# Attention of an encoder layer: from a planner's order to one order written by hand

## The chip, the cores and the metric

The kernel runs on one core of a Trainium2 chip. The metric is device time in microseconds of one launch. All matrix products of the attention are fp32r; large values are split into a high part (rounded to fp32r) and a low part (the rest), and three products of parts stand for one exact product.

## The reference

One layer for two groups: a prompt of 2048 frames and a sample of 8 streams with 16 new frames and 1024 cached frames each. Cut to what matters here:

```python
h = rmsnorm(x, norm1_g) * (1 + scale) + shift
z = h @ w_in                                  # conv columns u_a, u_g; q, k, v; forget gate f
u = u_a * sigmoid(u_g)
q, k = rmsnorm(q, q_norm_g), rmsnorm(k, k_norm_g)     # per head: 8 heads of 64
logf = log_sigmoid(f + b_f)
# attention, causal, for the prompt and (with the cache) for the sample
s = q @ k.T * 64 ** -0.5 + (cum_q[:, None] - cum_k[None, :])     # cum = cumsum(logf)
attn = softmax(where(k_pos <= q_pos, s, -1e30)) @ v
# convolution branch: causal depthwise conv, width 31, then LayerNorm over channels and swish
conv_out = silu((y - mean(y)) * rsqrt(var(y) + eps) * ln_g + ln_b)
x = x + g1 * (concat([conv_out, attn]) @ w_out)
x = x + g2 * ((silu(h2 @ w_gate) * (h2 @ w_up)) @ w_down)        # h2: a second modulated rmsnorm of x
```

## The kernel before

The program goes through `project_u_v` (to about 400 us), `project_q_k` (to about 600), `attention` (608 to 1215), `project_out`, and the feed-forward part (from about 1250). A planner orders each engine's instructions: it lists those that can run, by priority (the order in which the program states them, moved by `later`), on a timeline of its own. SyncE (SP) issues most transfers; POOL issued those of keys and queries for the attention.

The attention has 4 head pairs `p` and 4 query blocks `qb` of 512 frames: 16 steps. A step has 4 (qb + 1) key tiles of 128 frames, two heads each; one key tile for one head is a unit, 320 units in all (24 in the first two steps). A unit: two score matmuls into a bank `s` (three banks, tag `u`; lines 948 and 949), a mask matmul on the diagonal (951), an exp on ScalarE (953) into `ef`, the high part `e` on ScalarE (1131, called from `parts_of`), the low part on VectorE or, every third, on POOL (1132), and later three value matmuls into `pv` (939). A column of the value tile that holds ones gives the softmax's sum in the same bank.

The softmax needs each query's maximum before the exp. `score_maxima` computes it ahead: one matmul into a bank `mx` (two banks, tag `cv`; 909, mask 911) and one reduction on VectorE (912) for each query tile and key block, 320 in all. `spread_maxima` transposes a step's maxima (923) and writes them as extra rows of the query operand `Q2` (925), so that the score matmul subtracts them. 32 maxima are computed during `project_q_k`, and later ones up to 48 units ahead.

At a step's end ScalarE copies value and sum out of the banks (970, 971), Ln and Exp give a reciprocal (973, 974), three operations of VectorE refine it and scale the value (975 to 977), and SP writes it to `cat_d` (978). `load` brings the next step's queries and values; a value load `vraw` (883) takes a slot of the ring `ef`.

Beside that runs `background`: the convolution's norm over 5 chunks of frames (`conv_norm`; VectorE's lines 727, 742 and the Newton steps 93 to 95, transfers 708 and 744) and the sample group's attention over 8 streams (`sample_setup` with a bias write of all streams, 1022; `sample_batch`). It uses one PSUM bank, `lane`, and starts after two steps. `weave` deals out these generators in proportion to given counts; a part that `take` runs with a positive `by` has a later priority. `last_parts` finishes the last block of queries and keys (`finish`; the transfers `q_d<-qp` and `k_d<-qp`).

Of the kernel before, what the change touches and what calls it, by code (L numbers as in the profile page):

```python
# [6 lines left out]
F32 = mybir.dt.float32  # L7
# [40 lines left out]
LEAD = 48  # L48
FIRST = 2
BACK = 0.85  # L50
MAXIMA_BY, BACK_BY = -300, 1000
# [66 lines left out]
class Layer:  # L118
# [583 lines left out]
    def conv_norm(self, ch, sp, bank):  # L702
# [7 lines left out]
        def channel_mean(src):  # L710
            pm = bank
            for j in range(4):
                nc.tensor.matmul(pm[32 * j:32 * j + 32, :n], self.ones[:, 0:32], src[j], start=True, stop=True,
                                 tile_position=(0, 32 * j))
            m = sp.tile([P, 512], F32, tag="cm", name="cm")
            nc.scalar.copy(m[:, :n], pm[:, :n])
            po = bank
            nc.tensor.matmul(po[:, :n], self.mean, m[:, :n], start=True, stop=True)
            return po

        mu = channel_mean([y[:, j, :n] for j in range(4)])
        ms = sp.tile([P, 512], F32, tag="cw", name="cmu")
        nc.scalar.copy(ms[:, :n], mu[:, :n])
        yield
        sqs = []
        for j in range(4):
            nc.vector.tensor_tensor(y[:, j, :n], y[:, j, :n], ms[:, :n], ALU.subtract)
            sq = sp.tile([P, 512], F32, tag="cq", name="cq", bufs=4)
            nc.scalar.activation(sq[:, :n], y[:, j, :n], AF.Square)
            sqs.append(sq[:, :n])  # L730
        yield
        var = channel_mean(sqs)
        v = sp.tile([P, 512], F32, tag="cv", name="cvar")[:, :n]
        nc.vector.tensor_scalar(v, var[:, :n], EPS, None, ALU.add)
# [3 lines left out]
        newton_rsqrt(nc, r, sp.tile([P, 512], F32, tag="cm", name="ct")[:, :n], v, 2)  # L738
        yield
        for j in range(4):  # L740
            z = y[:, j, :n]
            nc.vector.tensor_tensor(z, z, r, ALU.mult)
        yield
# [3 lines left out]
    def operands(self):  # L747

        nc, a = self.nc, self.a
        self.bm = self.cst.tile([P, 2, 4], F32, name="bm")  # L750
        nc.sync.dma_start(self.bm, a["bm"])
# [4 lines left out]
        for k, r, v in (("v", slice(AUX, AUX + 8), -1.0), ("t", slice(HD, HD + 2), 1.0)):  # L756
# [16 lines left out]
        yield from self.take(self.maxima_of_all, AHEAD)  # L773

    def attention(self, ctx):
# [4 lines left out]
        self.split3 = 0  # L780
# [5 lines left out]
        for t in self.Vt:  # L786
            for i in range(2):
                nc.scalar.activation(t[:, i, :, 1, :], self.ones[:, 0:HD].unsqueeze(1).broadcast_to([P, 4, HD]), AF.Copy, scale=1.0 - i)
        self.lf_bank = "cv"
        self.after_attention = ctx  # L790
        self.eslots, self.ecount = [(self.awk, f"e{i}") for i in range(5)], 0
        back = self.background()
        nback, done, units, scored = 15 + 5 * 7 + 1 + 8 * 11, 0, 0, AHEAD
        total = sum(8 * (qb + 1) for _, qb in STEPS)
        self.V = {}
        drain(self.load(0))

        for n, (p, qb) in enumerate(STEPS):
            parts = [(self.attend(p, qb, n), 8 * (qb + 1))]
            if n + 1 < len(STEPS):  # L800
                parts.append((self.load(n + 1), 4))
            if n == 0:
                parts.append((self.last_parts(), 12))
            units += 8 * (qb + 1)
            k = units + LEAD - scored
            parts.append((self.take(self.maxima_of_all, k, MAXIMA_BY), k))
            scored += k
            if n >= FIRST:
                k = int(nback * (units - quiet) / (total - quiet) / BACK) + 1 - done
                parts.append((self.take(back, k, BACK_BY), k))  # L810
                done += k
            else:
                quiet = units
            weave(*parts)
        drain(back)

    def take(self, gen, k, by=0):

# [808 lines left out]
```

## Time and profile before

| | |
|---|---|
| runs | 2849.34 us median of 3 (2840.97 to 2852.43) |
| profiled execution | 2841.08 us, span 2839.3, mean granted TensorE clock 0.977 |
| busy in the span | TensorE 96%, VectorE 76%, ScalarE 51%, POOL 18% |
| attention, 608 to 1215 us | TensorE 560.5 of 607 us, VectorE 467.4, ScalarE 427.2, POOL 177.5; clock 0.94 |

In the profile PE is TensorE's matmul, PEld its weight load, DVE VectorE, ACT ScalarE, SP SyncE; a q behind the name is the engine's queue. A row by stretch gives from:to, its length, busy us of each engine with its instruction count, the clock, the share of the DMA engines' time, and GB/s. A row by line gives busy us and mean ns of one, then the idle time of its engine just before it and what ended that. A row of waits gives total us, times and the longest.

### The profile page before, as it was taken

What the parts mean: (1) busy time and instruction counts of PE and PEld (TensorE: products, weight loads), DVE (VectorE), ACT (ScalarE), POOL (GpSimd) and SP (SyncE); (2) the same over time, 40 slices, a digit from 0 to 9 for tenths busy, and PEclk for the clock granted to TensorE, in tenths of its full rate; (3) what the DMA queues carried; (4) which work ended last, traced back from release to release, by engine and by line L of the source; (5) the groups of instructions that cost most, each with busy time, mean ns of one, the idle gap of its engine ahead of it and who ended that gap; (6) DMA issues with size and microseconds to landing.
All of it is one profiled execution on the core that took longest, in us unless ns stands there. A gap on an engine that the chain in (4) does not pass through costs nothing.

```text
span 2839.3 us, 48486 instructions
## 1 busy us (share of the span) xinstructions
PE 2731.4 (96%) x16536; PEld 2525.9 (89%) x16536; DVE 2158.0 (76%) x4235; ACT 1436.9 (51%) x2812; POOL 503.2 (18%) x685
## 2 busy tenths in 40 slices
PE   7999999999988999989998999999999999999999
PEld 6899988866666777789998999999999999999999
DVE  3698898988886888644488899777787778676765
ACT  4543323357675777754354445444454446555552
POOL 3454412243222232213212110000000000000000
PEclk9999999989898999999998999999999999999999
DMA  8753567673346656264667678776786669788873
GB/s 306 258 188 110 187 212 265 187 203 114 82 115 178 188 184 192 87 234 143 213 239 257 216 262 291 251 228 206 233 293 212 218 208 309 247 277 258 280 249 117
DMA packets 390024, 603.23 MB, mean 212 GB/s; under 512 B 46240, under 2 KB 249152, under 8 KB 387728
## 3 DMA queue, kind: packets, MB, share of 16 engines
q1 hardware_dynamic: 375312, 574.72, 62.3%
q0 software_dynamic: 14464, 25.42, 3.7%
q8 instruction: 130, 2.13, 0.3%
q14 instruction: 118, 0.97, 0.1%
HBM read 421.97 MB, written 178.07 MB: 211 GB/s over the span
## 4 chain that ended last, share of the span: by engine, by line
PE 78%; DMA 9%; DVE 5%; issue 4%; ACT 2%; POOL 1%; SPq 1%; POOLq 0%; ACTq 0%; DVEq 0%
PE z L1412 44%; PE z L509 7%; PE pv L939 5%; PE acc L1115 4%; PE pa L319 3%; PE pvv L339 3%; PE pg L319 3%; PE s L948 2%; PE s L949 2%; PE mx L909 2%; DMA vraw<-o_v 1%; DVE M L912 1%; DMA k_d<-qp 1%; PE pu L319 1%; DMA wraw<-w_in 1%
## 5 line engine op out<-in xcount | busy, mean ns | idle before, releaser
L1412 PE MATMUL z<-rT,rW 128*128 128x360 f32 (+1 forms) x8316 | 1382.0, 328 | 4.3 <-ACT oR L1214 2.0
L1412 PEld LDWEIGHTS z<-rT,rW 128*128 128x128 f32 x8316 | 1378.9, 188 | 5.9 <-ACT oR L1214 2.4
L1131 ACT ACTIVATE rW<-rR 128x512 fp32r<-128x512 f32 x714 | 436.1, 618 | 386.4 <-PE z L1412 294.9
L1132 DVE TENSOR_TENSOR rW<-rR,rW 128x512 fp32r<-128x512 f32 x714 | 480.7, 678 | 150.5 <-ACT rW L1131 147.3
L697 DVE SCALAR_TENSOR_TENSOR cv<-cu,cpar,cv 128x384 f32<-128x384 f32 x580 | 311.7, 618 | 2.0 <-ACT cv L695 1.6
L939 PE MATMUL pv<-e,V 128*128 128x512 f32 (+3 forms) x960 | 264.3, 381 | 20.5 <-ACT e L1131 11.4
L912 DVE TENSOR_REDUCE M<-mx 128x1 f32<-128x512 f32 (+2 forms) x320 | 190.2, 606 | 50.5 <-PE mx L909 34.2
L939 PEld LDWEIGHTS pv<-e,V 128*128 128x128 f32 x960 | 168.6, 192 | 64.6 <-ACT e L1131 12.3
L953 ACT ACTIVATE ef<-s 128x512 f32<-128x512 f32 (+3 forms) x320 | 166.3, 530 | 107.0 <-PE s L949 49.2
L509 PE MATMUL z<-hqx,wqh 128*128 128x384 f32 (+1 forms) x768 | 196.5, 333 | 0.8 <-DVE logf L346 0.8
L1131 ACT ACTIVATE rT<-traw 128x360 fp32r<-128x360 f32 (+1 forms) x315 | 149.7, 503 | 89.0 <-DMA traw<-gt_d 58.1
L1132 DVE TENSOR_TENSOR rT<-traw,rT 128x360 fp32r<-128x360 f32 (+1 forms) x315 | 158.6, 537 | 44.9 <-ACT rT L1131 44.6
L1132 POOL TENSOR_TENSOR e<-ef,e 128x512 fp32r<-128x512 f32 (+3 forms) x106 | 128.1, 1209 | 361.8 <-ACT e L1131 170.5
L1132 DVE TENSOR_TENSOR e<-ef,e 128x512 fp32r<-128x512 f32 (+3 forms) x214 | 147.9, 701 | 42.9 <-ACT e L1131 41.6
L1131 ACT ACTIVATE e<-ef 128x512 fp32r<-128x512 f32 (+3 forms) x320 | 175.0, 567 | 4.6
L509 PEld LDWEIGHTS z<-hqx,wqh 128*128 128x128 f32 x768 | 135.7, 188 | 18.7 <-issue 15.5
L909 PE MATMUL mx<-K,Q 96*128 96x512 f32 (+2 forms) x320 | 135.1, 431 | 15.2 <-DVE M L912 12.9
L1115 PE MATMUL acc<-ch,woh 128*128 128x360 f32 (+1 forms) x384 | 122.6, 338 | 16.1 <-ACT ch L1131 8.2
L1340 DVE TENSOR_TENSOR rR<-rR 128x512 f32<-128x512 f32 (+1 forms) x136 | 93.1, 705 | 54.9 <-DMA rR<-w_down 50.6
L948 PE MATMUL s<-Q,K 128*128 128x512 f32 (+3 forms) x320 | 127.3, 399 | 1.9 <-ACT ef L953 1.8
L1115 PE MATMUL acc<-ch,wol 128*128 128x360 f32 (+1 forms) x384 | 127.7, 336 | 0.0
L509 PE MATMUL z<-hqx,wql 128*128 128x384 f32 (+1 forms) x384 | 126.4, 329 | 0.0
(306 smaller groups left out, 3958.7 us busy)
## 6 DMA issues: line engine op xcount, KB each, us to landing
rR<-sup_d SPq DMA_DIRECT2D x176, 256.0 KB
rR<-w_gate SPq DMA_DIRECT2D x132, 256.0 KB
traw<-gt_d SPq DMA_DIRECT2D x154, 180.0 KB
rR<-w_down SPq DMA_DIRECT2D x104, 256.0 KB
rR<-sdn_d SPq DMA_DIRECT2D x96, 256.0 KB
rR<-w_up SPq DMA_DIRECT2D x88, 256.0 KB
sup_d<-rR SPq DMA_DIRECT2D x88, 256.0 KB
wa<-w_ada SPq DMA_DIRECT2D x16, 1024.0 KB
```

The source lines that it names most:

```text
L319: nc.tensor.matmul(pz[:, :n], w[:, m], x[:, :n], start=(c == 0 and k == 0), stop=(c == CB - 1 and k == 2))
L509: nc.tensor.matmul(z[:, :n], w[:, m], x[:, :n], start=(c == 0 and k == 0), stop=(c == CB - 1 and k == 2))
L697: self.pin(nc.vector.scalar_tensor_tensor(dst, src, w, acc[i], ALU.mult, ALU.add))
L909: nc.tensor.matmul(mx[:, :w], Q2[0:AUX, h, j * P:(j + 1) * P], K2[kb][0:AUX, h, :w], start=True, stop=not diag)
L912: nc.vector.tensor_reduce(M[:, i, kb:kb + 1], mx[:, :w], AX.X, ALU.max)
L939: nc.tensor.matmul(z[h][:, off:], V[kt // 4][:, v, kt % 4, h:h + 2, :].rearrange("p b c -> p (b c)"), e[:, x, off:], start=(kt == 0 and i ...
L948: nc.tensor.matmul(s[:, off:], K1[kb][:, h, sl], Q1[:, h, off:], start=True, stop=False)
L953: nc.scalar.activation(ef[:, off:], s[:, off:], AF.Exp)
L1115: self.nc.tensor.matmul(z[:, :n], w[:, m], y, start=(first and i == 0 and k == 0), stop=(last and i == len(terms) - 1 and k == 2))
L1131: self.nc.scalar.activation(hi, raw, AF.Copy)
L1132: engine.tensor_tensor(lo, raw, f32(hi), ALU.subtract)
L1412: nc.tensor.matmul(z, W[:, x, m], t[:, y, :w], start=(k == 0 and i == 0), stop=(k == n - 1 and i == 2))
```

## The change

The four compute engines follow the order in which the program states the attention; SP stays with the planner. The loop goes over units: scores and exp of unit u, one maximum (two until 44 are ahead), the low part of unit u - 1, the values of unit u - 5 (u - 2 in the first 25 units), one step of each finishing block, and the side work's due parts. The side work is cut into 266 parts (it has new `yield`s) and starts after 24 units; in these, the last block of `project_q_k` is finished.

A step's end is a generator, `normalize`: ScalarE copies the two banks whole (`zc`), moves the sums to the other half of the partitions by two transfers on its own queue, and three of the remaining multiplies and the write to `cat_d` go to POOL. The maxima reach `Q2` by a copy of 8 rows and 8 transfers of one row instead of two products with `bm`; K then has one row of -1 instead of eight. Keys and queries are loaded on SP. Value loads have a slot of their own (`vr`). There are 4 + 4 slots `e` instead of 5 + 3, and three cache slots `kv` for keys and values of the sample instead of two and two. The convolution's last taps are issued before the stream.

```diff
-LEAD = 48
-FIRST = 2
-BACK = 0.85
-MAXIMA_BY, BACK_BY = -300, 1000
+LEAD = 44
+FIRST = 24
+BACK = 266
+ENGINES = {mybir.EngineType.PE, mybir.EngineType.Activation, mybir.EngineType.DVE, mybir.EngineType.Pool}
...
     def attention(self, ctx):
...
-        back = self.background()
...
-        for n, (p, qb) in enumerate(STEPS):
-            parts = [(self.attend(p, qb, n), 8 * (qb + 1))]
...
-            weave(*parts)
-        drain(back)
+        self.conv_part(999, TT)
+        drain(self.load(0))
+        with self.tc.manual_schedule(engines=ENGINES):
+            self.stream()
+
+    def stream(self):
+        units = [(n, p, qb, kt, h) for n, (p, qb) in enumerate(STEPS) for kt in range(4 * qb + 4) for h in range(2)]
+        back = self.background()
+        scored, done, ended, late = AHEAD, 0, None, None
+        for u, (n, p, qb, kt, h) in enumerate(units):
+            if kt == h == 0:
+                step = (p, qb, self.V[p], [])
+                loads = self.load(n + 1) if n + 1 < len(STEPS) else iter(())
+            ef, off, e = self.scores(n, p, qb, kt, h)
+            for _ in range(2):
+                if scored < u + 1 + LEAD:
+                    next(self.maxima_of_all, 0)
+                    scored += 1
+            if late:
+                self.low_part(*late)
+            late = (e[:, 1, off:], ef[:, off:], f32(e[:, 0, off:]))
+            self.waiting.append((step, kt, h, off, e))
+            while len(self.waiting) > len(self.eslots) // 2 + (u > FIRST):
+                self.value(*self.waiting.pop(0))
+            for g in self.finishing[:]:
+                if next(g, 1):
+                    self.finishing.remove(g)
+            if kt % (2 * qb + 2) == 1 and h == 0:
+                next(loads, 0)
+            if u < FIRST:
+                self.parts(0, TT)
+            else:
+                while not ended and done < BACK * (u - FIRST) / (len(units) - FIRST - 8):
+                    ended = next(back, 1)
+                    done += 1
...
     def keys(self, p):
...
-            nc.gpsimd.dma_start(K2[0:HD + 2], rows[HD:])
+            nc.sync.dma_start(f32(K2[0:HD + 2]), rows[HD:])
...
     def spread_maxima(self, Z, Q2):
...
-        for h in range(2):
-            nc.vector.tensor_tensor(Q2[r, h, :].rearrange("r (j q) -> r j q", j=4),
-                                    pz[r, :].unsqueeze(1).broadcast_to([8, 4, P]),
-                                    self.bm[r, h, :].unsqueeze(2).broadcast_to([8, 4, P]), ALU.mult)
+        yield
+        m = self.lp.tile([P, P], F32R, tag="mrow", name="mrow", bufs=2)
+        nc.vector.tensor_copy(m[r], pz[r])
+        for i in range(8):
+            nc.sync.dma_start(f32(Q2[AUX:AUX + 1, i // 4, i % 4 * P:(i % 4 + 1) * P]), f32(m[AUX + i:AUX + i + 1]))
+        yield
...
+    def normalize(self, p, qb, zc):
+        nc, wk = self.nc, self.awk
+        sm, r = (wk.tile([P, 512], F32, tag=k, name=k, bufs=1) for k in ("sm", "rs"))
         for h in range(2):
             o, x = slice(HD * h, HD * h + HD), slice(HD - HD * h, P - HD * h)
-            nc.scalar.copy(sm[o], z[h][x])
-            nc.scalar.copy(pvs[o], z[h][o])
...
+            nc.scalar.dma_start(sm[o], zc[x, h])
+            yield
+        yield
+        nc.scalar.activation(r, sm, AF.Ln, scale=-1.0)
         self.last_exp = nc.scalar.activation(r, r, AF.Exp, scale=-1.0)
-        nc.vector.tensor_tensor(sm, sm, r, ALU.mult)
-        nc.vector.scalar_tensor_tensor(sm, sm, 2.0, r, ALU.subtract, ALU.mult)
-        nc.vector.scalar_tensor_tensor(pvs, pvs, -1.0, sm, ALU.mult, ALU.mult)
-        nc.sync.dma_start(self.cat_d[:, 4 + p, qb * 512:(qb + 1) * 512], pvs)
+        yield
+        nc.gpsimd.tensor_tensor(sm, sm, r, ALU.mult)
+        yield
+        yield
+        nc.vector.scalar_tensor_tensor(r, sm, 2.0, r, ALU.add, ALU.mult)
+        yield
+        for h in range(2):
+            o = slice(HD * h, HD * h + HD)
+            nc.gpsimd.tensor_tensor(zc[o, h], zc[o, h], r[o], ALU.mult)
+            nc.gpsimd.dma_start(self.cat_d[o, 4 + p, qb * 512:(qb + 1) * 512], zc[o, h])
...
     def sample_batch(self, b, bank):
...
             if c < 2:
-                kt = self.smc.tile([P, NP, 512], F32, tag="kc", name="kc")
+                kt = self.smc.tile([P, 4 * DC], F32, tag="kv", name="kc").rearrange("p (g k) -> p g k", g=NP)
                 nc.sync.dma_start(kt, a["kcT"][b, :, :, c0:c0 + w])
```

More of the change, by code (lines that the diff above doesn't have):

```diff
@@ L737, in conv_norm @@
         nc.scalar.activation(r, r, AF.Exp, scale=-0.5)
[L738 removed]
         yield
+        for _ in range(2):
+            newton_rsqrt(nc, r, sp.tile([P, 512], F32, tag="cm", name="ct")[:, :n], v, 1)
+            yield
         for j in range(4):
@@ L772, in operands @@
         self.maxima_of_all = self.score_maxima()
-        yield from self.take(self.maxima_of_all, AHEAD)
+        for _ in range(AHEAD):
+            next(self.maxima_of_all)
+            yield
     def attention(self, ctx):
@@ L815, in attention @@
-        drain(back)
-    def take(self, gen, k, by=0):
-        for _ in range(k):
-            with later(self.tc, by):
-                end = next(gen, 1)
-            if end:
-                return
-            yield
-    def last_parts(self):
-        while self.todo:
-            self.parts(0, TT)
-            yield
+        self.eslots, self.ecount = [(self.awk, f"e{i}") for i in range(4)], 0
+        self.V, self.finishing = {}, []
+        self.conv_part(999, TT)
+        drain(self.load(0))
@@ new lines, in attention @@
+        with self.tc.manual_schedule(engines=ENGINES):
+            self.stream()
+    def stream(self):
+        units = [(n, p, qb, kt, h) for n, (p, qb) in enumerate(STEPS) for kt in range(4 * qb + 4) for h in range(2)]
+        back = self.background()
+        scored, done, ended, late = AHEAD, 0, None, None
[4 more added lines that the diff above has]
+            ef, off, e = self.scores(n, p, qb, kt, h)
+            for _ in range(2):
+                if scored < u + 1 + LEAD:
[14 more added lines that the diff above has]
+                self.parts(0, TT)
+            else:
+                while not ended and done < BACK * (u - FIRST) / (len(units) - FIRST - 8):
+                    ended = next(back, 1)
+                    done += 1
+        self.low_part(*late)
+        for w in self.waiting:
+            self.value(*w)
+        for g in self.finishing:
+            drain(g)
+        assert ended or next(back, 1), "parts are left"
@@ new lines, in value @@
+    def value(self, step, kt, h, off, e):
+        nc = self.nc
+        p, qb, V, z = step
+        last = kt == 4 * qb + 3
+        if kt == 0:
+            z.append(self.bank("tr", "pv"))
+        for i, (v, x) in enumerate(((0, 0), (0, 1), (1, 0))):
+            nc.tensor.matmul(z[h][:, off:], V[kt // 4][:, v, kt % 4, h:h + 2, :].rearrange("p b c -> p (b c)"), e[:, x, off:],
+                             start=(kt == 0 and i == 0), stop=(last and i == 2))
+        if last:
+            if h == 0:
+                self.zc = self.awk.tile([P, 2, 512], F32, tag="zc", name="zc", bufs=1)
+            nc.scalar.copy(self.zc[:, h], z[h])
+            if h:
+                self.finishing.append(self.normalize(p, qb, self.zc))
```

191 lines of the change are left out of this document (85 added, 106 removed).

## The prediction

> **What bounds the kernel now.** I read the page first: TensorE is busy 96% of the span, so a gain must come from a stage in which this figure hides waiting. The change touches one stage, the attention, from the first score matmul at 608.1 us to the last value matmul at 1212.5. Next I read busy time by stretch of time, for all instructions and for one line that runs once in each unit (a key tile times a query block of one head; 320 in all). The cuts are where the other work changes: before the convolution's norm (24 units done), during it (104 units), from the sample group on (192 units). The changed code cuts nearly there too: its side work starts after unit 24 and 95 of its 266 parts are the norm's.
>
> ```profile
> PE 2731.4 (96%) x16536; PEld 2525.9 (89%) x16536; DVE 2158.0 (76%) x4235; ACT 1436.9 (51%) x2812; POOL 503.2 (18%) x685
> ```
>
> All instructions by stretch, then line 949 (second score matmul), the sample and norm bank `lane`, and line 912 (the maxima's reduction):
>
> ```profile
> core 0: us, PE busy (x) PEld busy (x) DVE busy (x) ACT busy (x) POOL busy (x), PEclk, DMA share, GB/s
> 608.00:662.00 54.00, 48.92 (x192) 34.30 (x192) 44.53 (x75) 33.62 (x75) 28.36 (x32) 0.82 0.71 191
> 662.00:871.00 209.00, 187.91 (x825) 132.76 (x824) 173.65 (x293) 145.03 (x289) 57.51 (x53) 0.93 0.30 86
> 871.00:1215.00 344.00, 323.70 (x2153) 245.18 (x2152) 249.17 (x444) 248.54 (x491) 91.62 (x88) 0.96 0.57 172
> 950.00:1200.00 250.00, 245.29 (x1764) 184.26 (x1764) 194.82 (x339) 192.25 (x385) 67.76 (x64) 1.00 0.52 163
> ...
> 662.00:871.00 209.00, 40.77 (x104) 21.12 (x104) 0.93 0.30 86
> 871.00:1215.00 344.00, 71.48 (x192) 36.67 (x192) 0.96 0.57 172
> 950.00:1200.00 250.00, 53.01 (x145) 27.27 (x146) 1.00 0.52 163
> ...
> 662.00:871.00 209.00, 27.40 (x100) 6.46 (x100) 3.05 (x5) 7.82 (x15) 0.93 0.30 86
> 871.00:1215.00 344.00, 63.04 (x882) 33.74 (x882) 21.05 (x58) 11.34 (x24) 0.96 0.57 172
> ...
> 662.00:871.00 209.00, 67.83 (x113) 0.93 0.30 86
> 871.00:1215.00 344.00, 98.66 (x166) 0.96 0.57 172
> ```
>
> From 950 to 1200 TensorE is busy 98% at clock 1.00 and a unit takes 250/145 = 1.72 us. From 662 to 871 a unit takes 209/104 = 2.01 us, with the clock at 0.93 and no engine over 90%: there the stage waits. For the price of a unit I take a run of three value matmuls, and the score matmul's widths:
>
> ```profile
> 1085.91 0.86 PE L939 MATMUL pv<-e,V 128*128 128x512 f32 x3
> ...
> L939 PE MATMUL pv<-e,V x960: 218/392/792, 621.7 to 1212.5; 128*128 128x512 f32 x137, 128*128 128x256 f32 x20, 128*128 128x384 f32 x19, 128*128 128x128 f32 x16
> L948 PE MATMUL s<-Q,K x320: 220/393/800, 608.1 to 1210.6; 128*128 128x512 f32 x112, 128*128 128x384 f32 x16, 128*128 128x256 f32 x16, 128*128 128x128 f32 x16
> ```
>
> One record lasts 0.39 but the next starts (0.86 - 0.39)/2 = 0.235 us later. Widths of 512 (70%), 384, 256 and 128 (10% each) average 435 columns, so 0.20 us a matmul. A unit has two score and three value matmuls, 1.00, with masks 1.05 (estimate); a maximum costs 0.20, with its mask 0.22. The stage's TensorE work by pitch is then: start 24 x 1.05 + 29 x 0.22 = 32 of 54 us; norm 104 x 1.05 + 113 x 0.22 + 27.4 = 161 of 209; sample 192 x 1.05 + 166 x 0.22 + 63.0 = 301 of 344. So about 22 + 48 + 43 us of 607 are not work; the clock's missing shares (0.18, 0.07, 0.04 of the stretches) are 38 of these. The chain and the waits from 608 to 950 name what ends them:
>
> ```profile
> 621.16 7.09 DMA k_d<-qp
> 789.89 8.46 DMA vraw<-o_v
> 899.18 25.20 DMA vraw<-o_v
> 1218.86 5.85 DMA cat_d<-pvs
> ...
> PEld mx L909 <- DVE M L912: 26.9, 41, 2.8
> ACT V L1131 <- DMA vraw<-o_v: 21.8, 6, 12.6
> PE pv L939 <- ACT e L1131: 11.4, 2, 10.6
> ```
>
> Read: a value load sits in the exp's own ring (tag `ef`, three slots), so a late load holds a slot, ScalarE's split waits up to 12.6 us, and everything behind it in ScalarE's order waits too. The maxima wait for VectorE to empty their two banks.
>
> **The change part by part.** Rows for the prices:
>
> ```profile
> L1132 POOL TENSOR_TENSOR e<-ef,e 128x512 fp32r<-128x512 f32 (+3 forms) x106 | 128.1, 1209 | 361.8 <-ACT e L1131 170.5 <-PE mx L911 55.1 <-PE mx L909 21.3
> L1132 DVE TENSOR_TENSOR e<-ef,e 128x512 fp32r<-128x512 f32 (+3 forms) x214 | 147.9, 701 | 42.9 <-ACT e L1131 41.6
> L925 DVE TENSOR_TENSOR Q<-pz,bm 8x512 fp32r<-8x512 f32 x30 | 19.6, 691 | 2.2 <-PE pz L923 1.9
> L975 DVE TENSOR_TENSOR sm<-sm,rs 128x512 f32<-128x512 f32 x15 | 11.4, 759 | 1.3 <-ACT rs L974 1.1
> L977 DVE SCALAR_TENSOR_TENSOR pvs<-pvs,sm 128x512 f32<-128x512 f32 x15 | 10.2, 683 | 0.0
> L970 ACT COPY sm<-pv 64x512 f32<-64x512 f32 x32 | 18.6, 581 | 10.9 <-PE pv L939 10.3
> L93 DVE SCALAR_TENSOR_TENSOR ct<-cr 128x512 f32<-128x512 f32 (+1 forms) x10 | 7.6, 757 | 0.1
> L1131 ACT ACTIVATE e<-ef 128x512 fp32r<-128x512 f32 (+3 forms) x320 | 175.0, 567 | 4.6
> L953 ACT ACTIVATE ef<-s 128x512 f32<-128x512 f32 (+3 forms) x320 | 166.3, 530 | 107.0 <-PE s L949 49.2 <-PE s L951 24.0 <-DVE e L1132 21.7
> ...
> L1132 DVE TENSOR_TENSOR e<-ef,e x214: 276/681/2440, 611.2 to 1211.8; 128x512 fp32r<-128x512 f32 x75, 128x384 fp32r<-128x384 f32 x12, 128x128 fp32r<-128x128 f32 x10, 128x256 fp32r<-128x256 f32 x10
> L697 DVE SCALAR_TENSOR_TENSOR cu<-uS,cpar,ca x4: 345/348/352, 568.2 to 600.4; 128x128 f32<-128x128 f32 x4
> ...
> Q<-q_d POOLq DMA_DIRECT2D x14, 512.0 KB, 4.7
> K<-k_d POOLq DMA_DIRECT2D x13, 512.0 KB, 6.0
> K<-k_d POOLq DMA_DIRECT2D x11, 264.0 KB, 5.5
> bias_d<-bias SPq DMA_DIRECT2D x1, 4160.0 KB
> ...
> SPq L744 <- DVE cy L742: 88.4, 5, 31.1
> 1096.36 0.34 SPq L978 DMA_DIRECT2D cat_d<-pvs  x1
> ```
>
> *Order.* TensorE, ScalarE, VectorE and POOL follow the written order; SP's queue does not. A unit issues scores, exp, high part, one maximum (two until 44 ahead), the low part of the unit before, the values of five units back, at most one step of a finishing block, 0.92 side parts. Behind each possible wait there is slack: three score banks, two maxima banks, eight `e` slots. ScalarE's and VectorE's latencies for a unit (means of 0.53 and 0.57 for exp and high part, 0.70 or 1.21 for the low part) sum to 2.3 us, against five units of 1.5 us.
>
> *Value load in its own slot.* The 21.8 us of ScalarE's wait goes, provided SP issues the load a step early; late next is VectorE.
>
> *Steps' ends.* Per step VectorE loses two mask products (2 x 0.69), 0.76 and 0.68, and gains one 8-row copy (0.2, estimate): 2.6 us less. ScalarE copies 2 x 0.58 in place of 4 x 0.58 and issues two transfers (0.34 each by SP's row): 0.5 less. POOL takes three multiplies (1.21 each) and two transfer issues; it has 57.5 of 209 us busy, so they hide under its idle time. They may hold VectorE up: its low part takes 0.68 at the median, 2.44 at the longest, and 0.70 in the mean although the mean width asks for 0.68 x 435/512 = 0.58; 214 x 0.12 = 26 us, some 0.2 for each of POOL's 106 low parts. I take 0.2 for each of the 48 new multiplies; bounds 0 and 1.21. Ln now waits for a transfer inside SBUF, two units after its issue.
>
> *Loads of K and Q on SP.* POOL loses 42 issues, SP gains them and 8 one-row transfers a step: 128 x 0.34 = 44 us of queue time, beside work of other engines as long as nothing in front waits. But SP does wait for others (88.4 us on the norm's results), and what stands behind waits too.
>
> *Side work in 266 parts.* Same instructions, but each part ends where another engine must act, so an in-order engine rarely waits for it. VectorE's lumps stay: a Newton part is three operations of 0.76.
>
> *Small things.* The ring of three shared cache slots in place of four, the convolution drained before the stream (its last instruction runs at 600.4 already), one row of -1 in K, signs turned: nothing on the path; if the cache ring is late, a part waits for 1 MB, as in 871 to 950 now.
>
> **The sum.** *Start*: 36 maxima in place of 29, the same chain through `k_d` (7.09): 54 us kept; bounds 45 (VectorE's busy time there now) and 62 (the 7.09 once more). *Norm*: TensorE 104 x 1.05 + 104 x 0.22 + 27.4 = 159. VectorE 173.65, less 9 maxima (0.60 each, 67.83/113) and less 2.6 x 6 to 7 steps: 151. ScalarE 145 less 3. Three engines within 12% of each other in a fixed order leave no room for lumps: six Newton operations and four products behind them, at 0.76 each, put 7.6 us on VectorE in four units, beside 1.06 of its own in each (0.60 and 147.9/320), where TensorE offers 4 x 159/104 = 6.1; of the 5.7 us over, two banks absorb some 2.5; with four large chunks 13 us, and 18 multiplies of POOL at 0.2 make 4: 176, say 177. Bounds: 159 (all hidden) and 209 (as now). *Sample*: 192 x 1.05 + 148 x 0.22 + 63.0 = 297; at the present best rate 192 x 1.72 = 330, less 18 maxima, 326. I take 312, between them: 297, 5 of switching and 10 for one event. The 4160 KB bias write is issued in unit 134; the key block needed by the maximum of unit 140 gets its slot after unit 135 and now queues behind that write (before, on another queue). The value load that stood behind it took 25.20; 5 units are 7.7. So 0 to 18 us late; 10. *Tail*: the step's end is longer by a transfer (4.7 by Q's median) and POOL's products, but only the last two token blocks need it, and SP no longer stands on `cat_d<-pvs` (5.85): 0, bounds -6 and +6.
>
> 54 + 177 + 312 = 543 for 607: 64 us less. The profiled execution took 2841.08 (span 2839.3), 8 below the median 2849.34 and at the lowest run, 2840.97; 2841 - 64 = 2777, and runs of the new kernel should spread likewise: **2780 us**.
>
> Two rules of the Trainium skill bear on the steps' ends. "DMA: Bandwidth & Descriptors", section "Anatomy of one DMA", gives a transfer about 2.0 us of fixed cost plus its bytes at 436 GB/s, so 2.3 us for the 128 KB inside SBUF (an estimate from that page); by that rule Ln, 3.2 us later, never waits, and the slower case below has no price. By the trace's medians of 4.7 to 6.0 Ln waits up to 2.8 us a step, 45 in all, beside three score banks and an idle fifth of ScalarE's time (248.54 of 312); the sum stands by both. "SBUF — State Buffer", section "Who interferes with whom", says that a VectorE instruction with two SBUF inputs contends with a GpSimd instruction that reads SBUF, and that the later one is blocked for the whole of the other; by that rule the upper bound of 1.21 would hold, which is a rival below. The trace's longest of 2.44 agrees, its median of 0.68 does not show it as the rule.
>
> **The rivals.**
> *The floor is reached* (chance 0.20). Start 45, norm 165, sample 300: 510, so 2744. For it: half of the loss is the clock, which returns when gaps are short (1.00 from 950 on). Against: VectorE's lumps.
> *SP's queue takes back half* (0.15). Three late key blocks and three query blocks each have four units of slack, 6 to 7 us, against landings of 5.5 to 6.0 plus what SP waits for in front; 4 us each and 25.2 - 7.7 for the bias write make 42, of which 10 are in the sum: 2812. For it: SP's 88.4. Against: the planner still orders SP's queue by need.
> *POOL shuts VectorE out* (0.08). At 1.21 for each of 18 multiplies VectorE loses 22 us in the norm stretch, not 4: 195 there, and nothing in the sample stretch, where VectorE has 249 of 312: 2780 + 18 = 2798. For it: the 2.44. Against: the mean excess is a tenth of that.
> *It doesn't do what it says* (0.10). The order was never the limit; VectorE stays at 83% in the norm stretch and the sample stretch keeps 1.72 us a unit less its maxima: 54 + 209 + 337 = 600: 2834.
> *Slower* (0.11). Ln waits on ScalarE, in order, for the copy inside SBUF; all exps queue behind it, and three score banks (4.8 us) run dry. Each step then costs landing - 3.2 - 4.8. With 16 steps the gain is gone at a landing of 12 us and the kernel slower by over 0.5% from 13; at 14 it is 2780 + 96 = 2876. For it: 25.20 and 8.46 in the chain. Against: the medians of 4.7 to 6.0, and a queue that nothing else uses.
>
> **How the numbers follow.** The forecast holds 0.36, with a range of its own of 2755 to 2800. A measurement of this kernel tells 0.5% (14 us) from no change. Faster: 0.36 + 0.20 + 0.15 + 0.08 = 0.79; same 0.10; slower 0.11. For 8 in 10 the range is 2735 to 2850: it leaves out the slower case and the lower end of the floor case.
>
> **What would show it.** In the new profile: no wait of ScalarE for `vraw` over 3 us; VectorE's rows for the step's ends gone, POOL's 48 multiplies instead; 104 units from the first `cy` load in some 177 us with VectorE over 85%; granted clock near 1.00 in that stretch; one gap of TensorE of about 10 us near the bias write, ended by K. Wrong if ScalarE's wait for `sm` sums to over 60 us, if TensorE's waits for K or Q sum to over 40, or if the norm stretch keeps over 200 us.

## Result: 4.1% slower

The changed kernel takes 2963.34 us (median of 4, 2959.98 to 2967.66) where the kernel before takes 2846.73 (median of 4): ratio 1.0413, interval 1.0396 to 1.0430. That is 117 us more, where 64 less were forecast. The profiled execution has a span of 2965.9 us.

The profile after. First the page's line of busy time, then the attention by stretch: start, norm, sample, cut at the first load of `cy` and at the end of the last norm chunk. Columns as in the prediction; below them the second score matmul (now line 961) in the same stretches.

```profile
PE 2757.3 (93%) x16536; PEld 2541.1 (86%) x16536; DVE 2129.8 (72%) x4187; ACT 1434.7 (48%) x2780; POOL 544.6 (18%) x701
...
608.00:671.00 63.00, 57.05 (x158) 39.13 (x157) 42.09 (x78) 24.52 (x53) 18.14 (x20) 0.54 0.49 131
671.00:928.00 257.00, 196.95 (x869) 144.91 (x868) 175.41 (x286) 153.58 (x297) 78.35 (x68) 0.85 0.28 82
928.00:1338.00 410.00, 332.86 (x2137) 243.25 (x2135) 219.66 (x397) 248.88 (x468) 121.22 (x109) 0.91 0.50 149
...
608.00:671.00 63.00, 8.02 (x16) 4.57 (x15) 0.54 0.49 131
671.00:928.00 257.00, 43.81 (x112) 23.39 (x112) 0.85 0.28 82
928.00:1338.00 410.00, 73.67 (x192) 38.22 (x192) 0.91 0.50 149
```

The stage takes 730 us, not 607, and idle TensorE time is 730 - 586.86 = 143 us, before 607 - 560.5 = 46.5. The clock's missing shares are 29 + 39 + 37 = 105 us, before 38. The norm stretch holds 112 units in 257 us, 2.29 each (before 2.01); the 192 units of the sample stretch take 2.14 each (before 1.79). No engine is near its limit: VectorE has 175 of 257 us. So the stage now waits more than before, and the waits say where. The first row is of before, the rest of after, over the attention (a `lane` product is one of the side work):

```profile
PE lane L713 <- DMA cy<-y_d: 2.6, 1, 2.6
...
PE lane L712 <- DMA cy<-y_d: 30.3, 4, 8.7
PE lane L1079 <- DVE S L1082: 27.1, 7, 22.4
DVE S L1082 <- DMA S<-bias_d: 21.9, 1, 21.9
ACT zc L984 <- DMA cat_d<-zc: 16.3, 3, 6.5
PE pv L979 <- ACT zc L984: 8.7, 2, 4.5
PE lane L1107 <- ACT pT L1104: 12.3, 8, 6.5
PE lane L1101 <- ACT pT L1104: 9.8, 8, 2.2
PE lane L1101 <- ACT S L1094: 9.1, 6, 2.8
```

TensorE itself stands before the side work's products, in front of everything the written order has behind them: four times for a chunk of the convolution's results, once for 22.4 us for the sample's bias, and 22 times for a result of ScalarE (31 us, the last three rows). All the idle time of TensorE that the traces show before `lane` products in the attention is 103 of the 143 us; before, it was 6. Of the 103, 36 end with a transfer, 35 with a result of ScalarE and 32 with one of VectorE, the bias's 22.4 among these. The stop for the bias in order of time:

```profile
957.65 0.58 SPq L1058 DMA_DIRECT2D bias_d<-bias  x1
982.24 0.81 SPq L1066 DMA_DIRECT2D S<-bias_d  x2
988.55 1.94 PE L1079 MATMUL lane<-kc,Qbd 128*32 128x512 f32 x8 [22.37 <-DVE S L1082]
```

The read of the bias is issued 24.6 us after the write, VectorE's addition waits for it, the bank `lane` waits for VectorE, and TensorE's next product waits for the bank.

### The profile page after: what moved, and what is told of

Read it like the earlier page. It is cut to its first block, busy times and chain, and to the rows that moved or that the text cites. A ratio compares the mean times of both kernels' runs of the same rounds, so it can differ in the third digit from the quotient of the medians.

```text
span 2965.9 us, 48688 instructions
## 1 busy us (share of the span) xinstructions
PE 2757.3 (93%) x16536; PEld 2541.1 (86%) x16536; DVE 2129.8 (72%) x4187; ACT 1434.7 (48%) x2780; POOL 544.6 (18%) x701
## 5 line engine op out<-in xcount | busy, mean ns | idle before, releaser
L979 PE MATMUL pv<-e,V 128*128 128x512 f32 (+2 forms) x960 | 274.9, 397 | 11.6 <-ACT zc L984 8.7
L979 PEld LDWEIGHTS pv<-e,V 128*128 128x128 f32 x960 | 182.6, 208 | 44.4 <-ACT zc L984 10.5
L969 ACT ACTIVATE e<-ef 128x512 fp32r<-128x512 f32 (+3 forms) x320 | 181.5, 567 | 10.5 <-PE pv L979 0.3
L960 PE MATMUL s<-Q,K 128*128 128x512 f32 (+3 forms) x320 | 141.7, 443 | 0.0
L961 PE MATMUL s<-Q,K 128*128 128x512 f32 (+3 forms) x320 | 125.9, 393 | 2.0 <-DMA Q<-mrow 2.0
```

The source lines that it names most:

```text
L960: nc.tensor.matmul(s[:, off:], K1[kb][:, h, sl], Q1[:, h, off:], start=True, stop=False)
L969: nc.scalar.activation(e[:, 0, off:], ef[:, off:], AF.Copy)
L979: nc.tensor.matmul(z[h][:, off:], V[kt // 4][:, v, kt % 4, h:h + 2, :].rearrange("p b c -> p (b c)"), e[:, x, off:], start=(kt == 0 and i ...
```

## Experiments

Theory A: a written order turns each late load of the side work into a stop of TensorE, and the stop costs half clock on top. Rivals: B, the stream's own order is too tight; D, the new pieces cost it (step's end, transfers), not the order; E, the order of the other engines; C, the clock alone; H and F come up below. "Ratio" is to runs of the kernel before beside each set; their medians lie between 2842 and 2847 us, so differences of some 5 us between sets say little.

**The order taken away.**

```diff
-        with self.tc.manual_schedule(engines=ENGINES):
-            self.stream()
+        self.stream()
```

> The new kernel with the fixed order taken away: the same pieces, the same five-behind values and the same transfers, but the four compute engines are given back to the planner. Theory A (in the fixed order TensorE stands in front of matmuls of the side work whose loads have not landed, 30 us for the convolution's results and 22 us for the sample's bias, and runs at half clock after each stop): the planner puts other work in front, so 2790 to 2860, at most the time of the kernel before. Theory D (not the order but the new pieces cost the time: the step's end over transfers and POOL, Q's rows by eight transfers, the single zc slot): still over 2920.

Measured: 2854.51, ratio 1.0039 (1.0022 to 1.0055). Of the loss, 2963.34 - 2854.51 = 109 us is the order; the new pieces under the planner are some 10 us slower than the kernel before. The last unit is scored at 1212 us, before at 1211. D falls.

**The old kernel in a fixed order.**

```diff
+        with self.tc.manual_schedule(engines=ENGINES):
+            for n, (p, qb) in enumerate(STEPS):
...
+                weave(*parts)
```

> The kernel before with one part of the change: the four compute engines follow its written order in the attention, where the planner had moved its pieces. Theory A and E together (a fixed order on in-order engines turns every late load and every late result of another engine into a stop for all that stands behind): slower by 100 us or more, 2945 to 3060. Rival H (the loss lies in how the new stream places its parts, not in fixing an order): under 2900.

Measured: 3167.61, ratio 1.1139 (1.1116 to 1.1162): fixing the old order costs 323 us, over 100 more than the forecast allowed. Here the maxima stand right behind their own query load:

```profile
PE mx L911 <- DMA Q<-q_d: 116.9, 12, 16.2
```

So the new stream is the far better order to fix (109 us), but neither reaches the planner. H falls.

**The stream alone, side parts behind it.**

```diff
-                while not ended and done < BACK * (u - FIRST) / (len(units) - FIRST - 8):
-                    ended = next(back, 1)
-                    done += 1
+                if not done:
+                    next(back)
+                    done = 1
...
+        drain(back)
```

> The new kernel with its first side part at unit 24 and all other side parts after the last unit, so the stream of scores, maxima and values runs alone and the side work alone behind it. The whole gets longer; what counts is the time from the first to the last value matmul. By matmul pitch the stream alone is 320 x 1.05 + 288 x 0.22 = 399 us. Theory A: units run at 1.3 to 1.5 us from unit 24 on, 450 to 490 us for the stream, with the clock near 1.00 after the start. Theory B (the written order of the stream's own pieces is too tight: two maxima banks, ScalarE's exp, VectorE): 1.8 us a unit or more, over 560 us. In both the first 24 units stay at half clock, some 63 us.

```profile
671.00:1108.00 437.00, 403.97 (x2018) 335.09 (x2016) 316.97 (x519) 353.74 (x678) 197.68 (x175) 0.97 0.26 70
...
671.00:1108.00 437.00, 111.57 (x304) 57.78 (x304) 0.97 0.26 70
...
ACT zc L984 <- DMA cat_d<-zc: 18.9, 3, 7.1
```

By the profile, stream and start end at 1108 us, some 500 after the first score (450 to 490 forecast); from 671 us on it is 437/304 = 1.44 us a unit, as forecast, clock 0.97. With the side work between, the same 304 units take 667 us (671 to 1338): 230 us more for side work that has 25.81 + 66.20 = 92 us of TensorE's busy time (rows below). B falls: the five-behind stream runs well by itself. (Its transfers and its time on the other engines are gone with the side work, so the 230 us do not price the order alone.) The longest wait for a transfer that it keeps is `zc`'s: a single slot whose write has not landed when the next short step ends. (The whole took 3062.15, with the side work at the end; one run.)

```profile
671.00:928.00 257.00, 25.81 (x100) 6.19 (x100) 3.00 (x5) 7.61 (x15) 0.85 0.28 82
928.00:1338.00 410.00, 66.20 (x882) 31.30 (x882) 21.01 (x58) 11.02 (x24) 0.91 0.50 149
```

**Whose order.** Each time one engine, or three, went back to the planner. For TensorE, and likewise for the others:

```diff
-ENGINES = {mybir.EngineType.PE, mybir.EngineType.Activation, mybir.EngineType.DVE, mybir.EngineType.Pool}
+ENGINES = {mybir.EngineType.Activation, mybir.EngineType.DVE, mybir.EngineType.Pool}
```

> The new kernel with TensorE alone given back to the planner; ScalarE, VectorE and POOL keep the written order. Theory A (it is TensorE's place in the written order, in front of products that wait for a load or for another engine, that costs the 109 us between the fixed order and the planner): 2840 to 2890. Rival E (the fixed order of VectorE and ScalarE is what loses, TensorE only shows it): 2920 to 2980.

> The converse: TensorE alone keeps the written order, the planner has ScalarE, VectorE and POOL. Theory A: still 2930 to 2990, with the same four stops before the convolution's products and the one before the sample's. Rival E: back to 2840 to 2880.

> The changed kernel with VectorE alone given back to the planner; TensorE, ScalarE and POOL keep the written order. If VectorE's order is what the other engines' half of the loss is (lumps of the convolution's norm in front of the maxima's reductions, the prediction's own term): 2905 to 2930. If not: 2945 to 2965.

> The changed kernel with ScalarE alone given back to the planner. If ScalarE's order is the other engines' half of the loss (the copies at a step's end and Ln, which wait for transfers, in front of the exps): 2905 to 2930. If not: 2945 to 2965.

| under the planner | us | ratio (interval) | less than 2963.34 |
|---|---|---|---|
| TensorE | 2904.35 | 1.0219 (1.0198 to 1.0241) | 59 |
| VectorE, ScalarE, POOL | 2911.56 | 1.0246 (1.0219 to 1.0273) | 52 |
| VectorE | 2941.96 | 1.0335 (1.0315 to 1.0356) | 21 |
| ScalarE | 2942.29 | 1.0340 (1.0320 to 1.0360) | 21 |

59 + 52 = 111 against 109: the two halves add. TensorE's order is over half; VectorE's and ScalarE's, each freed alone, are a fifth each. 52 - 21 - 21 leaves some 10 for POOL's order or for what the three hold up together; that was not tried. All four times fell between the two ranges of their forecasts: A put nearly all on TensorE. With VectorE free, TensorE's loads are waited for longer (54.4 us, was 30.3) and the time still falls; waits of engines do not sum to time:

```profile
PE lane L712 <- DMA cy<-y_d: 54.4, 4, 16.4
```

**The loads earlier.** Two slots for the convolution's results, the load stated a chunk ahead (to make room, one small tile of the norm shares another's slot, not shown):

```diff
-        y = sp.tile([P, 4, 512], F32, tag="cy", name="cy")
-        nc.sync.dma_start(y[:, :, :n], self.y_d[:, :, t0:t0 + n])
+        y = self.cys.pop(0)
+        if ch < 4:
+            self.conv_load(ch + 1, sp)
...
+    def conv_load(self, ch, sp):
+        n = 512 if ch < 4 else P
+        y = sp.tile([P, 4, 512], F32, tag="cy", name="cy", bufs=2)
+        self.nc.sync.dma_start(y[:, :, :n], self.y_d[:, :, ch * 512:ch * 512 + n])
+        self.cys.append(y)
```

> The new kernel with two slots for the convolution's results, each chunk's load stated when the chunk before it begins (the variance takes the mean's slot, to make room). Theory A: TensorE's four stops of 5.8 to 8.7 us (30.3 us) go, and of the 58 us at half clock around them the 28 that are not the stop itself, worth 14: 44 us less, 2915 to 2930. Theory B: the norm stretch is held by VectorE and the two maxima banks anyway, under 20 us less, 2945 to 2963.

Measured: 2925.99, ratio 1.0288 (1.0270 to 1.0307): 37 us less for stops of 30.3 us that are gone from the waits, as forecast. A holds for these. The same edit under the planner:

> The changed pieces under the planner, with two slots for the convolution's results. Theory A (the planner already puts other work in front of a late load): within 8 us of 2854, though the same edit gave 37 in the fixed order. Rival: it helps here as much, 2815 to 2825.

Measured: 2859.93, ratio 1.0054 (1.0032 to 1.0076): no gain, as forecast by A. The planner had covered these loads.

**Distance in the order**, on top of the two slots: empty parts behind the bias write (first line) and ahead of the gates' product.

```diff
-        for _ in range(4):
+        for _ in range(20):
             yield
...
-        yield
+        for _ in range(6):
+            yield
...
-BACK = 266
+BACK = 287
```

> The kernel with two slots for the convolution's results, and in addition distance in the written order: 20 empty parts in place of 4 between the bias write and the sample's first product, 6 in place of 1 ahead of the sample's first product of gates; 287 parts in all instead of 266. Theory A: of 2926 the stop of 22.4 us and that of 5.7 go, 2893 to 2903. Rival F (the side work's parts are now denser, and TensorE waits as much for the other engines): over 2915.

Measured: 2920.21, ratio 1.0275 (1.0252 to 1.0297): 6 us, which the intervals do not separate from nothing (1.0270 to 1.0307 with the two slots alone), not the 23 to 33 that A forecast. It lies in rival F's range. Both stops are gone, and others stand in their place. Four engine instructions in order of time, with the wait before each in brackets:

```profile
829.39 0.59 ACT L993 COPY zc<-pv 128x512 f32<-128x512 f32 x1 [7.47 <-DMA cat_d<-zc]
898.14 0.86 DVE L1033 COPY Qbd<-qS 64x512 f32<-64x512 f32 x2 [8.43 <-DMA qS<-qs_d]
938.91 0.63 ACT L1007 ACTIVATE rs<-sm 128x512 f32<-128x512 f32 x1 [7.36 <-DMA sm<-zc]
953.24 0.45 PE L936 MATMUL mx<-K,Q 96*128 96x128 f32 x1 [5.72 <-DMA K<-k_d]
```

Each is a late transfer, three of them on another engine than TensorE. The last two are the prediction's own mechanisms (Ln behind the copy inside SBUF, a key block behind the bias write). That the longer stop had covered them until then fits, but no run shows it. F has its share too: TensorE's waits for the maxima's reductions on VectorE rose from 17.0 to 26.3 us.

**The same with TensorE under the planner** (this edit and the one for TensorE above).

> TensorE under the planner, the other three in the written order, with two slots for the convolution's results and the distance of 20 and 6 empty parts. If the two losses (TensorE's order, the other engines' order) add, the loads' stops that are left there (9.4 us before the convolution's products, 18.6 before the sample's, and half clock behind them) go: 2868 to 2885. If the time is held by VectorE's and ScalarE's own order, 2895 to 2905.

Measured: 2869.31, ratio 1.0085 (1.0062 to 1.0108): 35 us under 2904.35, within the forecast. When the second score matmul of three units starts, by the traces in us, shows where each edit acts (units 24 to 127 are the norm's in the prediction, 128 to 319 the sample's):

| kernel | unit 24 | unit 128 | unit 319 | norm | sample |
|---|---|---|---|---|---|
| before | 675 | 881 | 1211 | 206 | 329 |
| after | 685 | 928 | 1336 | 243 | 407 |
| two slots | 681 | 889 | 1296 | 208 | 408 |
| and distance | 683 | 913 | 1295 | 229 | 382 |
| and TensorE planned | 679 | 898 | 1242 | 219 | 344 |

With its loads moved ahead the norm is as short as before. The distance takes 25 us out of the sample, nearly the forecast 28, and the units ahead of it, where the side work's parts are now denser, get 22 longer. TensorE's order is then still worth 51 us (2920.21 - 2869.31), 38 of them in the sample; TensorE's idle time before `lane` products falls with it from 40 to 15 us, and the 40 are all waits for results of ScalarE (30) and VectorE (10).

**The bias write cut in eight.**

```diff
-        nc.sync.dma_start(self.bias_d, bias[:n].unsqueeze(1).broadcast_to([n, QS, PAST + QS]))
+        for b in range(NS):
+            r = slice(b * H, (b + 1) * H)
+            nc.sync.dma_start(self.bias_d[r], bias[r].unsqueeze(1).broadcast_to([H, QS, PAST + QS]))
```

> The new kernel with the 4160 KB bias write cut into eight writes of 520 KB, one for each stream, so that the first stream's bias can be read when an eighth has landed. Theory A: TensorE's one stop of 22.4 us before the sample's first product shrinks to under 5 and the half-clock windows in it go: 2936 to 2948. Theory B or D: the stop only moves, within 5 us of 2963.

Measured: 2986.72, ratio 1.0495 (1.0473 to 1.0518): 23 us slower, the wrong way.

```profile
957.71 28.73 SPq L1060 DMA_DIRECT2D bias_d<-bias  x8
986.48 6.33 SPq L1068 DMA_DIRECT2D S<-bias_d  x1
...
PE lane L1081 <- DVE S L1084: 48.9, 1, 48.9
```

The eight issues hold SP's queue for 28.7 us (the one: 0.58), so the read is issued behind all eight, and its data come later still. The first two issues take 0.81 and 0.72 us, the other six 3.6 to 5.1. The transfers themselves are slow: while they run, the DMA engines are half busy and move 81 GB/s, where the one write keeps them 98% busy at 220 (after, then with eight writes):

```profile
963.00:982.00 19.00, 3.18 (x17) 2.30 (x13) 2.89 (x3) 2.72 (x5) 5.43 (x6) 0.69 0.98 220
...
962.00:986.00 24.00, 4.24 (x22) 2.45 (x21) 4.00 (x4) 3.78 (x7) 6.21 (x6) 0.67 0.51 81
```

So the edit made the bias later and says little on A. Why writes from 8 partitions are slow was not tried.

**The clock.** In the first 24 units it is at half without a break, though TensorE is busy: after, then three stretches of the first run below.

```profile
605.00:666.00 61.00, 53.82 (x141) 36.61 (x142) 40.19 (x77) 21.70 (x49) 15.40 (x19) 0.50 0.53 141
...
605.00:628.00 23.00, 19.59 (x54) 13.11 (x55) 17.10 (x32) 5.68 (x11) 5.00 (x5) 0.51 0.48 128
628.00:645.00 17.00, 14.24 (x68) 10.24 (x67) 13.12 (x26) 6.92 (x18) 4.85 (x7) 0.99 0.41 111
645.00:662.00 17.00, 15.54 (x39) 10.67 (x38) 8.79 (x18) 9.86 (x20) 6.61 (x7) 0.51 0.48 130
```

The burst, called with `times` 16 for unit 2:

```diff
+        for _ in range(times):
+            nc.tensor.matmul(s[:, off:], K1[kb][:, h, sl], Q1[:, h, off:], start=True, stop=_ < times - 1)
-        nc.tensor.matmul(s[:, off:], K1[kb][:, h, sl], Q1[:, h, off:], start=True, stop=False)
```

> The new kernel with the first score matmul of unit 2 issued 16 times (15 of them overwritten, so 15 x 512 columns of extra work, 6.4 us at half clock). Theory C (the clock stays at half from 605 to 666 us with hardly a gap because in each window of 3.4 us TensorE streams too few columns, about 0.7 of what half clock can; one full window releases it and it then stays released): the clock is 1.00 from about 620 on, the first 24 units take 50 to 54 us with the burst in place of 63, and the whole 2948 to 2957. Rival (the half clock comes from something else than the columns streamed in the window): the burst only adds its length, 2967 to 2972.

Measured: 2957.78, ratio 1.0409 (1.0383 to 1.0435), not told apart from the change without it. The clock was released at 628, as C has it, but fell again at 645, so C's second half (it stays released) fails; shortly before, at 640 to 642 us, TensorE waited 2.05 us for POOL's low part. Unit 24 was scored 6 us earlier (679, after 685), not 9 to 13. Filling the four stops:

```diff
         yield
         yield
+        self.fill(bank, 40 if ch else 0)
         quarter_means([y[:, j, :n] for j in range(4)])
...
+    def fill(self, bank, times):
+        for _ in range(times):
+            self.nc.tensor.matmul(bank[:, 0:3 * P].rearrange("p (i k) -> p i k", i=3), self.masks[:, 2], self.masks[:, 0:3], start=True, stop=True)
```

> The changed kernel with 40 matmuls of 384 columns on constants, results overwritten, before the first product on the convolution's results in chunks 1 to 4: 7 us of useless work where TensorE waits 5.8 to 8.7 us. The wait itself stays. Theory C (the clock is halved for a window of 3.4 us and those after it when a window streams too few columns): the half clock around these four stops (58 us, 28 of them outside the stops) goes, 10 to 14 us less, 2949 to 2954. Rival (what the stops cost is the waiting alone): 0 to 4 us more, 2963 to 2968.

Measured: 2957.06, ratio 1.0391 (1.0372 to 1.0409). From 727 to 902 us, after and with the fill:

```profile
727.00:902.00 175.00, 125.16 (x513) 90.20 (x514) 105.90 (x173) 92.93 (x178) 45.15 (x37) 0.79 0.32 95
727.00:902.00 175.00, 150.46 (x698) 117.41 (x698) 109.91 (x174) 97.80 (x189) 47.53 (x39) 0.91 0.32 95
```

The clock rises from 0.79 to 0.91, worth 21 us of full clock over the stretch, and the kernel gains 6, which the intervals do not separate from nothing (1.0372 to 1.0409 against 1.0396 to 1.0430). That is half the forecast at most. It fits half clock that lies beside waits for other engines and costs little of its own, but no run shows that by itself.

**The value load's slot, and the pieces under the planner.** The old kernel with a slot of its own for `vraw` and, for room, three shared cache slots; the ring alone; and the converse in the new pieces under the planner, without and with the side work ending 40 units early. In the old kernel (the ring alone has only the second pair, which stands for the keys', values' and gates' tiles), then in the new:

```diff
-        raw = self.awk.tile([P, 4, P], F32, tag="ef", name="vraw", bufs=3)
+        raw = self.awk.tile([P, 4, P], F32, tag="vr", name="vraw", bufs=1)
...
-                kt = self.smc.tile([P, NP, 512], F32, tag="kc", name="kc")
+                kt = self.smc.tile([P, 4 * DC], F32, tag="kv", name="kc").rearrange("p (g k) -> p g k", g=NP)
```
```diff
-        raw = self.awk.tile([P, 4, P], F32, tag="vr", name="vraw", bufs=1)
+        raw = self.awk.tile([P, 4, P], F32, tag="ef", name="vraw", bufs=3)
...
-                while not ended and done < BACK * (u - FIRST) / (len(units) - FIRST - 8):
+                while not ended and done < BACK * (u - FIRST) / (len(units) - FIRST - 40):
```

> The kernel before, planner and all, with one part of the change: the value load has a slot of its own instead of one of the exp's ring; to make room the sample's caches share three slots, as in the change. The prediction's step alone: ScalarE's waits of 21.8 us for the value load and TensorE's stop of 10.6 us behind the longest go, 2828 to 2837. Rival: the load is late by as much in its own slot, or the shared ring costs what is gained: 2840 to 2852.

> The kernel before, planner and all, with the sample's caches in three shared slots only; the value load is back in the exp's ring. It splits the 25 us that the two edits together had cost. If the shared ring costs it: 2860 to 2875. If the value load's own slot costs it (its load is issued at another time and the planner's whole order turns out otherwise): 2840 to 2850.

> The changed pieces under the planner, with the value load back in the exp's ring, as the kernel before has it: the converse of the run in which the old kernel got the slot and lost 25 us. If the slot itself costs it under the planner (a load that holds a slot of the ring also holds the order together): 2830 to 2843. If that loss was an accident of one planned order: within 8 us of 2854.

> The same, with the side work stated to end 40 units before the stream's end instead of 8. Under the planner the new pieces end the attention when the old ones do, at 1212 us, but the last stream of the sample is late there and stands in TensorE's way until 1225. If that is the 10 us by which the pieces under the planner lose to the kernel before: 8 to 12 us under p_ef, 2832 to 2846. Rival: the earlier side work takes TensorE's time from the units and nothing is gained, within 4 us of p_ef.

| kernel | us | ratio (interval) |
|---|---|---|
| old, own slot and ring | 2869.45 | 1.0097 (1.0074 to 1.0120) |
| old, ring alone | 2846.40 | 1.0015 (1.0002 to 1.0028) |
| new pieces planned, value load in the exp's ring | 2852.15 | 1.0032 (1.0018 to 1.0047) |
| the same, side work 40 units early | 2860.25 | 1.0062 (1.0047 to 1.0076) |

What `vraw` was waited for, in all engines, before and with its own slot:

```profile
  DMA vraw<-o_v: 28.1, 11
  DMA vraw<-o_v: 13.8, 4
```

In the old kernel the ring alone costs some 3 us, as forecast; with the own slot the wait halves and the time grows by 23 us more, outside both forecasts; in the new pieces the slot makes no difference (2852.15 with the ring, 2854.51 with the slot). So the slot's loss belongs to one planned order. What in that plan costs the 23 us stays open, and so does what the 10 us of the new pieces are: ending the side work earlier, forecast to win them back, cost 8 more. No version tried beats the kernel before.

## Why the prediction was wrong

**The step that failed** is "*Side work in 266 parts*": "each part ends where another engine must act, so an in-order engine rarely waits for it." TensorE did wait there: 103 of its 143 idle us in the attention lie before the side work's products, before the change 6. The step left out transfers. A part that begins with a load is followed, two parts later, by a product on TensorE that needs it, and 58 of the 103 us stand behind late transfers, 36 directly and 22.4 by way of VectorE. It also counted on the other engine being done when the next part comes, about one unit later; the other 44 us are waits for results of ScalarE and VectorE. What covered both was the planner (under it TensorE's idle time before the same products is 8 us), and the change removes it.

In time, the written order is 109 of the 117 us. The runs, one edit on top of the other, split it: 37 for the convolution's loads, 6 for distance (not clear of noise), 51 for TensorE's order that is left with these, and 15 (2869.31 against 2854.51) for the order of the other three engines. Which waits make up the 15 stays open, and no edit took the 51 apart. The same hole is in "*Order*", which weighed the slots of the stream's own pieces (rightly: 1.44 us a unit alone) and not what the side work puts among them.

**The sum, term by term.** Start: 54 us for 24 units, at most 62, was forecast; the last of them is scored at 684 us, 76 after 608 (before at 660), and unit 24 at 685 (before 675, after a gap). Half clock for 61 us was not foreseen. Norm: 177 forecast for 104 units; they took 243 (the stretch of 257 has 8 units more). VectorE, the forecast limit, is busy 68% of it, not over 85%, and VectorE's whole order is worth 21 us in the kernel, where lumps were given 13. Sample: 312 forecast, 410 measured by the stretch. The one event was put in the right place, the bias write, but on the key block behind it (10 us); it was the bias itself, read back behind the same write, 22.4. The key block came out only when that stop was gone (5.7). Tail: 0 forecast; from the last value matmul to the first of the output projection, TensorE's idle time went from 6.34 to 9.57, so 3.2 us more, within the forecast's bound of 6:

```profile
1219.09 2.82 PE L1115 MATMUL acc<-ch,woh 128*128 128x368 f32 x8 [6.34 <-ACT ch L1131]
1348.14 0.67 PE L1159 MATMUL acc<-ch,woh 128*128 128x368 f32 x1 [9.57 <-ACT ch L1175]
```

**What held.** The rows of after:

```profile
L1175 ACT ACTIVATE V<-vraw 128x512 fp32r<-128x512 f32 x16 | 9.8, 616 | 0.5 <-DMA vraw<-o_v 0.5
L998 ACT ACTIVATE rs<-sm 128x512 f32<-128x512 f32 x16 | 9.9, 618 | 7.0 <-DMA sm<-zc 7.0
L961 PE MATMUL s<-Q,K 128*128 128x512 f32 (+3 forms) x320 | 125.9, 393 | 2.0 <-DMA Q<-mrow 2.0
L854 DVE TENSOR_TENSOR e<-ef,e 128x512 fp32r<-128x512 f32 (+3 forms) x214 | 150.5, 703 | 51.7 <-ACT e L969 51.3
```

The wait for `vraw` is gone; under the planner that was no gain, and in the written order it was not tried by itself. Ln waits 7 us in all, in 4 of 16 steps and 3.9 at most. So the rival *Slower* had the direction right by luck: its reason was Ln's one transfer on ScalarE, and that is not where the time went. The estimate of 2.3 us, by which Ln never waits, rests on a fit that the Trainium skill ("DMA: Bandwidth & Descriptors", section "Anatomy of one DMA — SWDGE (gpsimd) path") gives for transfers that GpSimd issues; here ScalarE issues them. TensorE waits 2 us for the maxima's rows and for no key or query load, so their place on SP's queue was no limit. (By the trace of before POOL gave up 51 such issues, not 42; the sum does not use the number.) Of the prediction's own signs of being wrong only the norm stretch came, 257 us where 200 was the mark.

The term of 0.2 us for each of POOL's new multiplies was about right, though the low part's mean hides it (703 ns, before 701). A low part of full width takes 684 ns where no POOL operation overlaps it and 1116 in the mean of the 21 that overlap a new multiply. By an estimate from the trace (time over that of an undisturbed instruction of the same form), the 48 multiplies cost VectorE 15 us in the attention, 0.3 each, while POOL's own low parts cost it 8 us less than before. By the Trainium skill, "SBUF — State Buffer", section "Who interferes with whom", the later of two such instructions is blocked. The trace agrees: here the low part that starts 0.15 us after a multiply takes 1.69 us and ends 0.55 after it.

```profile
667.80 1.29 POOL L1001 TENSOR_TENSOR sm<-sm,rs 128x512 f32<-128x512 f32 x1 [1.05 <-ACT rs L999]
667.95 1.69 DVE L854 TENSOR_TENSOR e<-ef,e 128x512 fp32r<-128x512 f32 x1
```

**The clock** was taken as something that "returns when gaps are short". In the start it did not return in 61 us. The Trainium skill's "TensorE: Matmul & The Clock Gate", section "Part 1: The HAM clock gate (the "warmup" mystery)", says that a busy window of some 3.4 us releases it; here a profile's busy share of 53.82 in 61 us was not enough, and a burst of wide matmuls was.

## What to carry over

Before an order that a planner made is fixed by hand, list every transfer and every result of another engine that the written order reads, with the time until it is there and the units between issue and use; one without that distance stops every instruction behind it on its engine, whatever it belongs to. The price is to be read with the cover gone: the planned kernel showed 2.6 us of waiting for a load that cost 37 when the order was fixed. When one stop is cleared, others can take its place (28 us forecast, 6 measured), so read what else is late around the longest before forecasting its gain.

## What was unexpected in the hardware

- Eight broadcast writes of 520 KB from 8 partitions held SP's queue for 28.7 us and moved at 81 GB/s, one of 4160 KB from 64 held it for 0.58 and moved at 220.
- The granted clock was only 0.5 or 1, and changed only at multiples of 3.41 us (from 604.9 to 666.4 us after, 18 such steps at half). An estimate from the trace of after adds up, for each step in the attention, the columns of the matmuls started in it, narrower operands in proportion (rows and columns of the stationary one, out of 128). The 18 steps before a fall have at most 2,700 columns, the 17 before a return at least 2,600, the 45 others at half clock at most 3,100; of the 137 others at full clock, whose fullest has 7,700, five have under 3,100. In the start 17 steps have 700 to 2,800, and the one before the return has 4,000. It is no sharp rule: in the trace of before, steps with 1,400 columns kept full clock. A busy row of the profile does not show it: narrow matmuls and masks count as busy.
